# One encoder layer on one Trainium2 core: like turns of long and short matmuls joined, x brought in channel by channel, and the low weight parts laid 32 bytes further on

## The chip, the cores and the metric

The kernel runs on one core of one Trainium2 chip. The metric is the device time of one execution in microseconds (us). Before the change it is 1365.53 us, the median of 3 runs (1365.43 to 1365.78).

## What is computed

One layer over 256 tokens of 2048 channels in float32: RMSNorm, a bidirectional gated recurrence with its projections, RMSNorm and residual, then a gated feed-forward network with a width-3 convolution along the tokens, RMSNorm and residual. Cut to its matrix products and norms:

```python
h = rmsnorm(x, norm_pre_mix)                  # x: 256 x 2048
q, f_f, f_b, v, g = split(h @ w_in, 5)        # w_in: 2048 x 10240
o = recurrence_both_ways(silu(q), f_f, f_b, v)
m = (rmsnorm(o, g_norm) * silu(g)) @ w_out    # 2048 x 2048
x = x + rmsnorm(m, norm_post_mix)
h = rmsnorm(x, norm_pre_ffn)
up = dwconv3(h @ ffn_w_in, w_conv)            # 2048 x 11264
gate, val = split(up, 2)
x = x + rmsnorm((silu(gate) * val) @ ffn_w_out, norm_post_ffn)   # 5632 x 2048
```

## The kernel before, in words

**Weights and precision.** Every weight matrix is read once from HBM, in chunks of 512 output columns. A chunk comes in pieces of 4 tiles of 128 input rows (`raw`, 1 MB, line 115, issued on the SP queue) and is used in sub-chunks `s` of 2 such tiles (index `k`). Each float32 weight is split into two float32r parts: ScalarE rounds it to the high part `whi` (line 129), VectorE subtracts to get the low part `wlo` (line 130). `prep` does this three sub-chunks ahead (`LOOK`); four buffers of each part rotate, so a split waits until TensorE has finished with the sub-chunk four back. Activations are split alike: `xx[:, k, 0, :]` is the high and `xx[:, k, 1, :]` the low part of x for one tile of 128 channels and 256 tokens (`hh`, `oo` and `gg` are the same for later stages). A product is high by high, low by high and high by low.

**Two kinds of chunk.** `gemm` gives tokens as rows: the activations are the stationary operand, the weight parts move, and all its matmuls have 512 columns (lines 174, 177, 178). `gemm_t` gives channels as rows (the channel-row chunks: q and both f projections, and all but the first of the 22 up-projection chunks, 33 chunks in all): the weight parts are stationary. With the high weight part, both halves of the activation move at once, 512 columns (line 206, called **long** here); with the low weight part only the high half moves, 256 columns (line 209, **short**). A chunk has 64 long and 64 short ones. Before the change each of the first seven sub-chunks is a turn of 8 long and then 8 short matmuls, and the last one is four turns of 2 long and 2 short, so that the four output tiles are finished one after the other. The results collect in PSUM (`pg`, six banks) and are taken out by ScalarE and VectorE (lines 348, 349).

**The start.** SP issues a small parameter load, then pieces of x and of the first weights in turn (lines 247 to 260). x arrives with tokens as rows; TensorE transposes each tile of 128 by 128 (line 290, two for a tile of channels, 32 in all), ScalarE scales it by the norm weight into the high part (line 294), VectorE makes the low part (line 298). `split_x(0)` and `split_x(1)` stand ahead of the first chunk, the others between its sub-chunks. Ahead of all that, 18 transposes of the identity (line 269, `WARM`) keep TensorE busy. The mean square of x over channels is summed by ScalarE (8 squares with an accumulator, line 309), and spread over the partitions with two matmuls (`spread`, line 222).

**The order of the work.** A scheduler with a timeline model places the instructions on each engine, in-order queues; so the code's order is not always the queue's. Where two chunks meet, it mixes the last turns of one with the first of the next.

The lines that matter for the steps of the prediction: 115, 129, 130 (weights), 206, 209 (long, short), 269, 290, 294, 298 (start), 309 to 315 (mean square).

Of the kernel before, what the change touches and what calls it, by code (L numbers as in the profile page):

```python
# [11 lines left out]
F32 = mybir.dt.float32  # L12
F32R = mybir.dt.float32r
# [15 lines left out]
EPS = 1e-6  # L29
NLEV = 7  # L30
LOOK = 3
WARM = 18

ORDER = [(s, g) for g in range(NG - 1) for s in "qfbgv"][:-1]
ORDER += [("q", NG - 1), ("f", NG - 1), ("b", NG - 1), ("v", NG - 2), ("g", NG - 1), ("v", NG - 1)]
# [11 lines left out]
def encoder_layer(  # L47
    ctx: ExitStack,
    tc: tile.TileContext,
    x: bass.AP,  # L50
    w_in: bass.AP,
    w_o: bass.AP,
    w_up: bass.AP,
# [27 lines left out]
    r1 = const.tile([P, T], F32, name="rt", tag="rt")  # L81

    x_v = x.rearrange("(m p) d -> p m d", p=P)
    out_v = out.rearrange("(m p) d -> p m d", p=P)


# [31 lines left out]
    def prep(upto):  # L118
        while at["prep"] < min(upto, len(subs)):
            i = at["prep"]  # L120
            if at["load"] <= i:
                list(load())
            ci, s = subs[i]
            src = raws[ci, s // 2][:, 2 * (s % 2) : 2 * (s % 2) + 2, :]
            pl, sfx = (extra[0], str(s)) if ci == C_UP - 1 and s >= 2 * chunks[ci][2] - 4 else (wspl, "")
            hi = pl.tile([P, 2, 512], F32R, name="whi", tag="whi" + sfx)
            lo = pl.tile([P, 2, 512], F32R, name="wlo", tag="wlo" + sfx)
            for j in [slice(0, 1), slice(1, 2)] if i == 0 else [slice(0, 2)]:
                S.copy(hi[:, j], src[:, j])  # L129
                V.tensor_tensor(lo[:, j], src[:, j], hi[:, j].bitcast(F32), op=ALU.subtract)  # L130
            parts[ci, s] = (hi, lo)
            at["prep"] += 1
# [3 lines left out]
    def flush():  # L136
        while soon or later:
            step()
# [46 lines left out]
    def gemm_t(xx, need=None, pre=None):  # L185
# [4 lines left out]
        nsub = 2 * chunks[ci][2]  # L190
        base = subs.index((ci, 0))
        ps = [ps_g.tile([P, 2, T], F32, name="pg", tag="pg") for _ in range(4)]
        for s in range(nsub):
            if s == need:
                flush()
            if pre:
                pre(s)
            prep(base + s + (LOOK if ci else 1))
            hi, lo = parts[ci, s]


            tiles = [(n, 2 * s + j) for n in range(4) for j in range(2)]
            for run in [tiles] if s < nsub - 1 else [tiles[i : i + 2] for i in range(0, 8, 2)]:
                for n, k in run:
                    w = hi[:, k % 2, n * P : (n + 1) * P]
                    nc.tensor.matmul(ps[n], w, xx[:, k], start=(k == 0), stop=False)  # L206
                for n, k in run:
                    w = lo[:, k % 2, n * P : (n + 1) * P]
                    nc.tensor.matmul(ps[n][:, 0, :], w, xx[:, k, 0, :], start=False, stop=(k == 2 * nsub - 1))  # L209
            step()  # L210
        return ps

# [29 lines left out]
    hstack = ExitStack()  # L242
    sstack = ExitStack()
    spool = pool(sstack, "start", side="right")
    xs = spool.tile([P, 2, D], F32, name="xs")

    def load_x(a, b):
        nc.sync.dma_start(xs[:, :, a:b], x_v[:, :, a:b])

    nc.sync.dma_start(prm[:, :C_CW], par[:, :C_CW])  # L250
    load_x(0, 256)
    first = load(4)
    next(first), next(first)
    load_x(256, 512)
    list(first)
    load_x(512, 1024)
    list(load(2))
    load_x(1024, 1536)
    load_x(1536, 2048)
    make_identity(nc, ident)  # L260
    G.memset(mneg, -0.5)

# [20 lines left out]
    V.tensor_scalar(lb1, lb, -1.0, 1.0, op0=ALU.mult, op1=ALU.add)  # L283

    def split_x(k2):
        tp = ps_t.tile([P, 2, T], F32, name="tp", tag="tp")
        for j in range(2):
            k = 2 * k2 + j
            for m in range(2):
                nc.tensor.transpose(tp[:, j, m * P : (m + 1) * P], xs[:, m, k * P : (k + 1) * P], ident)  # L290
        for j in range(2):
            k = 2 * k2 + j
            w1 = prm[:, C_PRE + k : C_PRE + k + 1]
            S.activation(xx[:, k, 0, :], tp[:, j, :], AF.Copy, scale=w1)
        for j in range(2):
            k = 2 * k2 + j
            w1 = prm[:, C_PRE + k : C_PRE + k + 1]
            V.scalar_tensor_tensor(  # L298
                xx[:, k, 1, :], tp[:, j, :], w1, xx[:, k, 0, :].bitcast(F32), op0=ALU.mult, op1=ALU.subtract
            )  # L300

    ss1, rs1 = stile(8, "ss1"), stile(2, "rs1")

    def square_x(q):
        for m in range(2):
            jk = spool.tile([P, 512], F32, name="jk", tag="jk", bufs=2)
            i = 4 * m + q
            c = slice(q * 512, (q + 1) * 512)
            tc.keep_in_program_order(S.activation(jk, xs[:, m, c], AF.Square, accum_out=ss1[:, i : i + 1]))

    def mean_x():
        sx = stile(2, "sx")
        V.tensor_reduce(sx, ss1.rearrange("p (m q) -> p m q", q=4), axis=AX.X, op=ALU.add)
        rsqrt_mean(rs1, sx, D)
        soon.extend([nop, lambda: spread(rs1, r1)])

    split_x(0)
    split_x(1)
    ps0 = gemm_t(xx, pre=lambda s: split_x(s + 2) if 2 * s + 4 < KT else None)
    soon.extend([lambda q=q: square_x(q) for q in range(4)] + [mean_x])  # L320
    ps1 = gemm_t(xx)
    load_rest()
# [405 lines left out]
def _lay(inputs):  # L728
# [4 lines left out]
    def tiles(w):  # L733
# [17 lines left out]
    c = np.ascontiguousarray  # L751
    return {
        "x": c(f("x")[0]),
        "w_in": tiles(w_in),
        "w_o": tiles(w_o),
        "w_up": tiles(w_up),
# [21 lines left out]
```

## Time and profile before

| | |
|---|---|
| median of 3 runs | 1365.53 us |
| the profiled execution's own time | 1365.48 us |
| its span in the profile | 1363.7 us |
| TensorE matmuls | 7266, busy 1351.4 us (99%) |
| weight loads | 7266, busy 1167.3 us (86%) |
| VectorE, ScalarE busy | 955.5 us (70%), 698.0 us (51%) |
| HBM read | 245.63 MB, 182 GB/s over the span |
| mean granted TensorE clock | 0.998 |

The span is what the profile covers; 1.8 us of the execution's own time lie around it. A row of a timeline gives the start in us, the time from the first start to the last end, the engine (PE is TensorE's matmuls, PEld its weight loads, DVE VectorE, ACT ScalarE, POOL GpSimd, SPq the DMA queue of SyncE), the line, the operation, what it writes and reads, and how many in a row. The end of a matmul is modelled and reaches over the start of the next one, so the pace of a stream is read from one start to the next.

### The profile page before, as it was taken

The page shows a single profiled execution, that of the slowest core. Times are in us where ns is not written, and L with a number is a line of the kernel's source. Part 1 is how long each engine was busy: PE and PEld are TensorE (multiplying, and loading weights), DVE is VectorE, ACT ScalarE, POOL GpSimd, SP SyncE. Part 2 cuts the span into 40 slices and gives each one's busy share as a digit, 9 for nine tenths or more (in the row PEclk, how much of TensorE's full clock was granted, in tenths as well). Part 3 has the DMA queues.
Part 4 walks back from the last instruction along what each step waited for, and adds up shares of the span by engine and source line. Part 5 has one row for each costly group of instructions (what it writes and reads, how often), then busy time and mean ns, then how long its engine had stood idle before and what let it go on. Part 6 is the DMA issues. An engine that isn't in the chain of part 4 may idle for free.

```text
span 1363.7 us, 18236 instructions
## 1 busy us (share of the span) xinstructions
PE 1351.4 (99%) x7266; PEld 1167.3 (86%) x7266; DVE 955.5 (70%) x1204; ACT 698.0 (51%) x976; POOL 13.5 (1%) x21
## 2 busy tenths in 40 slices
PE   8999999999999999999999999999999999999997
PEld 7888988898898888888888888888888888888886
DVE  5688768876996887557767776777778675444444
ACT  5645545454545545547555555555555554434342
POOL 0000000000000000000000000000000000000000
PEclk9999999999999999999999999999999999999999
DMA  8554454445534534673555555555555556555552
GB/s 286 186 185 160 149 175 172 156 147 186 184 133 174 177 136 155 247 257 114 185 186 188 186 192 186 201 184 193 186 186 185 188 183 225 204 188 188 197 202 93
DMA packets 36997, 248.91 MB, mean 183 GB/s; under 512 B 4144, under 2 KB 4912, under 8 KB 7472
## 3 DMA queue, kind: packets, MB, share of 16 engines
q1 hardware_dynamic: 36912, 247.75, 51.8%
q8 instruction: 57, 0.93, 0.3%
q14 instruction: 28, 0.23, 0.0%
HBM read 245.63 MB, written 2.10 MB: 182 GB/s over the span
## 4 chain that ended last, share of the span: by engine, by line
PE 98%; DMA 1%; issue 0%; SPq 0%; DVE 0%; ACT 0%; DVEq 0%; POOLq 0%; POOL 0%
PE pg L206 35%; PE pg L209 18%; PE pg L174 13%; PE pg L178 13%; PE pg L177 13%; PE sc L462 3%; DMA raw<-in_w_in 1%; PE sc L428 1%; PE sc L519 1%; PE sc L487 1%; PE sc L518 1%; PE tp L233 0%; PE tp L614 0%; SPq L115 0%; DVE fw L715 0%
## 5 line engine op out<-in xcount | busy, mean ns | idle before, releaser
L130 DVE TENSOR_TENSOR wlo<-raw,whi 128x1024 fp32r<-128x1024 f32 (+1 forms) x457 | 556.3, 1221 | 342.2 <-ACT whi L129 334.4
L129 ACT CAST whi<-raw 128x1024 fp32r<-128x1024 f32 (+1 forms) x457 | 478.0, 1049 | 507.2 <-PE pg L178 227.1
L206 PE MATMUL pg<-hh,whi 128*128 128x512 f32 x1344 | 355.2, 393 | 0.0
L206 PEld LDWEIGHTS pg<-hh,whi 128*128 128x128 f32 x1344 | 234.1, 189 | 34.7
L209 PEld LDWEIGHTS pg<-hh,wlo 128*128 128x128 f32 x1344 | 197.4, 190 | 22.6
L206 PE MATMUL pg<-xx,whi 128*128 128x512 f32 x768 | 206.4, 397 | 0.3 <-DVE xx L298 0.3
L209 PE MATMUL pg<-hh,wlo 128*128 128x256 f32 x1344 | 203.3, 281 | 0.0
L206 PEld LDWEIGHTS pg<-xx,whi 128*128 128x128 f32 x768 | 134.8, 190 | 20.7 <-DVE xx L298 0.5
L174 PE MATMUL pg<-whi,gg 128*128 128x512 f32 x352 | 136.9, 389 | 0.0
L177 PE MATMUL pg<-wlo,gg 128*128 128x512 f32 x352 | 136.9, 389 | 0.0
L178 PE MATMUL pg<-whi,gg 128*128 128x512 f32 x352 | 136.9, 389 | 0.0
L209 PEld LDWEIGHTS pg<-xx,wlo 128*128 128x128 f32 x768 | 113.1, 190 | 12.3
L209 PE MATMUL pg<-xx,wlo 128*128 128x256 f32 x768 | 119.2, 283 | 0.0
L177 PE MATMUL pg<-wlo,xx 128*128 128x512 f32 x256 | 100.1, 391 | 0.0
L178 PE MATMUL pg<-whi,xx 128*128 128x512 f32 x256 | 100.0, 391 | 0.0
L174 PE MATMUL pg<-whi,xx 128*128 128x512 f32 x256 | 97.7, 390 | 0.0
L177 PEld LDWEIGHTS pg<-wlo,gg 128*128 128x128 f32 x352 | 66.1, 188 | 13.8
L178 PEld LDWEIGHTS pg<-whi,gg 128*128 128x128 f32 x352 | 66.1, 188 | 13.7
L174 PEld LDWEIGHTS pg<-whi,gg 128*128 128x128 f32 x352 | 66.1, 188 | 13.6
L178 PEld LDWEIGHTS pg<-whi,xx 128*128 128x128 f32 x256 | 48.1, 188 | 9.7
L177 PEld LDWEIGHTS pg<-wlo,xx 128*128 128x128 f32 x256 | 48.1, 188 | 9.8
L174 PEld LDWEIGHTS pg<-whi,xx 128*128 128x128 f32 x256 | 48.1, 188 | 9.7
(135 smaller groups left out, 1192.7 us busy)
## 6 DMA issues: line engine op xcount, KB each, us to landing
raw<-in_w_up SPq DMA_DIRECT2D x88, 1024.0 KB, 4.9
raw<-in_w_in SPq DMA_DIRECT2D x78, 1024.0 KB, 4.9
raw<-in_w_dn SPq DMA_DIRECT2D x44, 1024.0 KB, 4.9
raw<-in_w_o SPq DMA_DIRECT2D x16, 1024.0 KB, 4.9
x<-in_x SPq DMA_DIRECT2D x1, 2048.0 KB, 7.9
wp<-in_post SPq DMA_DIRECT2D x2, 1024.0 KB, 6.8
out<-fw SPq DMA_DIRECT2D x8, 256.0 KB, 2.6
xs<-in_x SPq DMA_DIRECT2D x3, 512.0 KB, 9.6
```

The costliest lines, as they stand in the source:

```text
L129: S.copy(hi[:, j], src[:, j])
L130: V.tensor_tensor(lo[:, j], src[:, j], hi[:, j].bitcast(F32), op=ALU.subtract)
L174: mm = nc.tensor.matmul(ps[m], a, hi[:, j, :], start=(k == 0), stop=False)
L177: nc.tensor.matmul(ps[m], a, lo[:, j, :], start=False, stop=False)
L178: nc.tensor.matmul(ps[m], b, hi[:, j, :], start=False, stop=(k == 2 * nsub - 1))
L206: nc.tensor.matmul(ps[n], w, xx[:, k], start=(k == 0), stop=False)
L209: nc.tensor.matmul(ps[n][:, 0, :], w, xx[:, k, 0, :], start=False, stop=(k == 2 * nsub - 1))
L428: nc.tensor.matmul(o, ones, a[:, i * 512 : i * 512 + 512], start=(j == 0), stop=(j == 1))
L462: nc.tensor.matmul(sc[:, j, :], kc[0][:, h, sl], r, start=True, stop=True)
L487: nc.tensor.matmul(sc[:, h, :], ks[:, d, h, s0 : s0 + P], qs[:, 1 - d, h, t0 : t0 + P], start=True, stop=True)
L518: nc.tensor.matmul(o[:, h, :], Sd[:, 2 * h + b, :], v[:, b, cs], start=True, stop=False)
L519: nc.tensor.matmul(o[:, h, :], So[1 - b][:, h, :], v[:, 1 - b, cs], start=False, stop=True)
```

## The change

The edits, in the order of the program:

- `WARM` goes from 18 to 24.
- The inputs have x a second time, laid out by channels on the host (`xt`: partition p holds channel 128k + p of every tile k, 256 tokens each). `xs` is loaded from it in pieces of tiles of channels (the same bytes as before), and `split_x` reads `xs` in SBUF: the 32 transposes of line 290 are gone. `split_x(0)` alone stands ahead of the first chunk; the others come between the sub-chunks, now behind `prep`.
- The mean square of x now has to be summed across partitions: four squares in place (ScalarE, 1024 elements a partition), four reductions over the 4 tiles of each and a fifth over the four results (VectorE), and two matmuls of one column with a vector of ones (TensorE).
- In `gemm_t` every second turn begins with its short matmuls, so that the short ones of two turns stand together, and then the long ones of the next two. In the first sub-chunk of all, the tiles go by `k`.
- The tile of the low weight part is 16 elements longer (4160 bytes in place of 4096), and in channel-row chunks the part begins 8 elements (32 bytes) in. This also moves what lies behind these tiles in SBUF.

```diff
-WARM = 18
+WARM = 24
...
-            lo = pl.tile([P, 2, 512], F32R, name="wlo", tag="wlo" + sfx)
+            lo = pl.tile([P, 1024 + 16], F32R, name="wlo", tag="wlo" + sfx)
+            o = 8 if ci < len(ORDER) and ORDER[ci][0] in "qfb" or C_UP < ci < C_UP + 2 * NJ else 0
+            lo = lo[:, o : o + 1024].rearrange("p (j n) -> p j n", n=512)
...
+        turn = [0]
         for s in range(nsub):
             if s == need:
                 flush()
+            prep(base + s + (LOOK if ci else 1))
             if pre:
                 pre(s)
-            prep(base + s + (LOOK if ci else 1))
             hi, lo = parts[ci, s]
             tiles = [(n, 2 * s + j) for n in range(4) for j in range(2)]
+            if ci == s == 0:
+                tiles.sort(key=lambda nk: nk[1])
             for run in [tiles] if s < nsub - 1 else [tiles[i : i + 2] for i in range(0, 8, 2)]:
-                for n, k in run:
-                    w = hi[:, k % 2, n * P : (n + 1) * P]
-                    nc.tensor.matmul(ps[n], w, xx[:, k], start=(k == 0), stop=False)
-                for n, k in run:
-                    w = lo[:, k % 2, n * P : (n + 1) * P]
-                    nc.tensor.matmul(ps[n][:, 0, :], w, xx[:, k, 0, :], start=False, stop=(k == 2 * nsub - 1))
+                long = turn[0] % 2 == 0
+                for kind in (long, not long):
+                    for n, k in run:
+                        w = (hi if kind else lo)[:, k % 2, n * P : (n + 1) * P]
+                        stop = s == nsub - 1 and kind != long and k == 2 * nsub - 1
+                        if kind:
+                            nc.tensor.matmul(ps[n], w, xx[:, k], start=(k == 0), stop=stop)
+                        else:
+                            nc.tensor.matmul(ps[n][:, 0, :], w, xx[:, k, 0, :], start=False, stop=stop)
+                turn[0] += 1
...
-    xs = spool.tile([P, 2, D], F32, name="xs")
+    xs = spool.tile([P, KT, T], F32, name="xs")
     def load_x(a, b):
-        nc.sync.dma_start(xs[:, :, a:b], x_v[:, :, a:b])
+        nc.sync.dma_start(xs[:, a:b], xt_v[:, a:b])
...
     def split_x(k2):
-        tp = ps_t.tile([P, 2, T], F32, name="tp", tag="tp")
...
+        for k in (2 * k2, 2 * k2 + 1):
+            S.activation(xx[:, k, 0, :], xs[:, k, :], AF.Copy, scale=prm[:, C_PRE + k : C_PRE + k + 1])
+        for k in (2 * k2, 2 * k2 + 1):
+            w1, hi = prm[:, C_PRE + k : C_PRE + k + 1], xx[:, k, 0, :].bitcast(F32)
+            V.scalar_tensor_tensor(xx[:, k, 1, :], xs[:, k, :], w1, hi, op0=ALU.mult, op1=ALU.subtract)
+    def square_x(q):
+        k = slice(4 * q, 4 * q + 4)
+        tc.keep_in_program_order(S.activation(xs[:, k], xs[:, k], AF.Square))
+        V.tensor_reduce(ss1[:, q, :], xs[:, k].rearrange("p k t -> p t k"), axis=AX.X, op=ALU.add)
+    def mean_x():
+        V.tensor_reduce(ss1[:, 4, :], ss1[:, :4].rearrange("p q t -> p t q"), axis=AX.X, op=ALU.add)
         tp = ps_t.tile([P, 2, T], F32, name="tp", tag="tp")
...
+            nc.tensor.matmul(tp[:, 0, m : m + 1], ss1[:, 4, m * P : (m + 1) * P], one, start=True, stop=True)
+        rsqrt_mean(rs1, tp[:, 0, :2], D)
...
     split_x(0)
-    split_x(1)
-    ps0 = gemm_t(xx, pre=lambda s: split_x(s + 2) if 2 * s + 4 < KT else None)
+    ps0 = gemm_t(xx, pre=lambda s: split_x(s + 1) if 2 * s + 2 < KT else None)
```

**What stands on TensorE at the start.** Before the change, from the first instruction on (`tp<-ident` are the warming transposes, `tp<-ident,xs` the transposes of x, `pg<-xx,whi` the long and `pg<-xx,wlo` the short matmuls of the first chunk):

```order
L269 MATMUL tp<-ident 128x128 x18
L290 MATMUL tp<-ident,xs 128x128 x8
L206 MATMUL pg<-xx,whi 128x512 x8
L209 MATMUL pg<-xx,wlo 128x256 x8
L206 MATMUL pg<-xx,whi 128x512 x8
L290 MATMUL tp<-ident,xs 128x128 x8
L209 MATMUL pg<-xx,wlo 128x256 x8
L206 MATMUL pg<-xx,whi 128x512 x4
L290 MATMUL tp<-ident,xs 128x128 x4
```

and after it:

```order
L283 MATMUL tp<-ident 128x128 x24
L220 MATMUL pg<-xx,whi 128x512 x8
L222 MATMUL pg<-xx,wlo 128x256 x16
L220 MATMUL pg<-xx,whi 128x512 x16
L222 MATMUL pg<-xx,wlo 128x256 x16
L220 MATMUL pg<-xx,whi 128x512 x16
```

The transposes of x have left the queue, and the second sub-chunk's short matmuls have moved ahead of its long ones.

**What stands on ScalarE at the start.** Before (`whi<-raw` is the high part of the weights, `xx<-tp` that of x, read from PSUM):

```order
L278 ACTIVATE lex<-lex 128x32
L129 CAST whi<-raw 128x512 x2
L294 ACTIVATE xx<-tp,prm 128x256 x4
L129 CAST whi<-raw 128x1024 x3
L294 ACTIVATE xx<-tp,prm 128x256 x6
L129 CAST whi<-raw 128x1024 x2
```

and after:

```order
L292 ACTIVATE lex<-lex 128x32
L301 ACTIVATE xx<-xs,prm 128x256 x2
L135 CAST whi<-raw 128x512 x2
L301 ACTIVATE xx<-xs,prm 128x256 x2
L135 CAST whi<-raw 128x1024
L301 ACTIVATE xx<-xs,prm 128x256 x4
L135 CAST whi<-raw 128x1024 x2
L301 ACTIVATE xx<-xs,prm 128x256 x8
```

x's high parts now stand ahead of the weights that they meet, eight of them ahead of the fifth sub-chunk's weights.

**What stands on TensorE in the middle of the up-projections.** Before, where two chunks meet and the plain turns of the second one begin (`hh` is the activation):

```order
L206 MATMUL pg<-hh,whi 128x512 x4
L209 MATMUL pg<-hh,wlo 128x256 x3
L206 MATMUL pg<-hh,whi 128x512 x4
L209 MATMUL pg<-hh,wlo 128x256 x4
L206 MATMUL pg<-hh,whi 128x512 x4
L209 MATMUL pg<-hh,wlo 128x256 x5
L206 MATMUL pg<-hh,whi 128x512 x8
L209 MATMUL pg<-hh,wlo 128x256 x8
```

and after, from the second run of a chunk to its last turns:

```order
L222 MATMUL pg<-hh,wlo 128x256 x8
L220 MATMUL pg<-hh,whi 128x512 x13
L222 MATMUL pg<-hh,wlo 128x256 x16
L220 MATMUL pg<-hh,whi 128x512 x16
L222 MATMUL pg<-hh,wlo 128x256 x16
L220 MATMUL pg<-hh,whi 128x512 x16
L222 MATMUL pg<-hh,wlo 128x256 x10
L220 MATMUL pg<-hh,whi 128x512 x4
L222 MATMUL pg<-hh,wlo 128x256 x4
```

Before, such a chunk has five runs of 8 and 8, four of 2 and 2, and four of about 4 and 4: 13 changes from short to long. After, its long runs are 7, 13, 16, 16, 4, 4 and 4: 7 changes.

More of the change, by code (lines that the diff above doesn't have):

```diff
@@ L50, in encoder_layer @@
     x: bass.AP,
+    xt: bass.AP,
     w_in: bass.AP,
@@ L83, in encoder_layer @@
     x_v = x.rearrange("(m p) d -> p m d", p=P)
+    xt_v = xt.rearrange("p (k t) -> p k t", t=T)
     out_v = out.rearrange("(m p) d -> p m d", p=P)
@@ L244, in encoder_layer @@
     spool = pool(sstack, "start", side="right")
-    xs = spool.tile([P, 2, D], F32, name="xs")
+    xs = spool.tile([P, KT, T], F32, name="xs")
     def load_x(a, b):
-        nc.sync.dma_start(xs[:, :, a:b], x_v[:, :, a:b])
+        nc.sync.dma_start(xs[:, a:b], xt_v[:, a:b])
     nc.sync.dma_start(prm[:, :C_CW], par[:, :C_CW])
-    load_x(0, 256)
+    load_x(0, 2)
     first = load(4)
     next(first), next(first)
-    load_x(256, 512)
+    load_x(2, 4)
     list(first)
-    load_x(512, 1024)
+    load_x(4, 8)
     list(load(2))
-    load_x(1024, 1536)
-    load_x(1536, 2048)
+    load_x(8, 12)
+    load_x(12, 16)
     make_identity(nc, ident)
@@ L285, in split_x @@
     def split_x(k2):
-        tp = ps_t.tile([P, 2, T], F32, name="tp", tag="tp")
[L287 to L300, printed above, removed]
@@ L302, in encoder_layer @@
-    ss1, rs1 = stile(8, "ss1"), stile(2, "rs1")
-    def square_x(q):
-        for m in range(2):
[L306 to L314, printed above, removed]
+        for k in (2 * k2, 2 * k2 + 1):
+            S.activation(xx[:, k, 0, :], xs[:, k, :], AF.Copy, scale=prm[:, C_PRE + k : C_PRE + k + 1])
@@ new lines, in split_x @@
+        for k in (2 * k2, 2 * k2 + 1):
+            w1, hi = prm[:, C_PRE + k : C_PRE + k + 1], xx[:, k, 0, :].bitcast(F32)
+            V.scalar_tensor_tensor(xx[:, k, 1, :], xs[:, k, :], w1, hi, op0=ALU.mult, op1=ALU.subtract)
+    ss1, rs1 = spool.tile([P, 5, T], F32, name="ss1"), stile(2, "rs1")
+    one = spool.tile([P, 1], F32, name="one")
+    G.memset(one, 1.0)
+    def square_x(q):
+        k = slice(4 * q, 4 * q + 4)
+        tc.keep_in_program_order(S.activation(xs[:, k], xs[:, k], AF.Square))
+        V.tensor_reduce(ss1[:, q, :], xs[:, k].rearrange("p k t -> p t k"), axis=AX.X, op=ALU.add)
@@ L753, in _lay @@
         "x": c(f("x")[0]),
+        "xt": c(f("x")[0].reshape(T, KT, P).transpose(2, 1, 0)).reshape(P, -1),
         "w_in": tiles(w_in),
```

## The prediction

> **What bounds the kernel now.** I read the page's busy table first, then the chain, then TensorE's timeline at the start and in the long stages.
>
> ```profile
> span 1363.7 us, 18236 instructions
> PE 1351.4 (99%) x7266; PEld 1167.3 (86%) x7266; DVE 955.5 (70%) x1204; ACT 698.0 (51%) x976; POOL 13.5 (1%) x21
> PE 98%; DMA 1%; issue 0%; SPq 0%; DVE 0%; ACT 0%; DVEq 0%; POOLq 0%; POOL 0%
> L130 DVE TENSOR_TENSOR wlo<-raw,whi 128x1024 fp32r<-128x1024 f32 (+1 forms) x457 | 556.3, 1221 | 342.2 <-ACT whi L129 334.4
> L129 ACT CAST whi<-raw 128x1024 fp32r<-128x1024 f32 (+1 forms) x457 | 478.0, 1049 | 507.2 <-PE pg L178 227.1
> ```
>
> The second row says that TensorE (PE) is busy 99% of the span, the third that 98% of the chain that ends last is TensorE's. The last two show the weight splits: VectorE's wait for ScalarE's, and ScalarE's wait for TensorE (227.1 us of their idle time for one line of its matmuls), not the reverse. So only two things can move the time: what TensorE does in a steady stream, and the start, where it waits. The start:
>
> ```profile
> 1.36 4.10 PE L269 MATMUL tp<-ident 128*128 128x128 f32 x18 [1.36 <-POOL ident masks.py:199]
> 1.64 0.93 SPq L115 DMA_DIRECT2D raw<-in_w_in  x2
> 2.62 0.43 SPq L248 DMA_DIRECT2D xs<-in_x  x1
> 5.25 0.87 PE L290 MATMUL tp<-ident,xs 128*128 128x128 f32 x4
> 6.11 1.31 ACT L129 CAST whi<-raw 128x512 fp32r<-128x512 f32 x2 [2.84 <-DMA raw<-in_w_in]
> 7.32 0.83 ACT L294 ACTIVATE xx<-tp,prm 128x256 fp32r<-128x256 f32 x2
> 8.67 0.63 PE L290 MATMUL tp<-ident,xs 128*128 128x128 f32 x4 [2.55 <-DMA xs<-in_x]
> 9.05 3.63 PE L206 MATMUL pg<-xx,whi 128*128 128x512 f32 x8
> 12.48 1.18 PE L209 MATMUL pg<-xx,wlo 128*128 128x256 f32 x8
> ...
> 13.54 1.05 ACT L129 CAST whi<-raw 128x1024 fp32r<-128x1024 f32 x1 [2.26 <-DMA raw<-in_w_in]
> 14.83 1.05 ACT L129 CAST whi<-raw 128x1024 fp32r<-128x1024 f32 x1 [0.24 <-DMA raw<-in_w_in]
> ...
> 23.23 1.12 PE L209 MATMUL pg<-xx,wlo 128*128 128x256 f32 x8
> 24.18 0.60 PE L290 MATMUL tp<-ident,xs 128*128 128x128 f32 x4
> 24.54 2.09 PE L206 MATMUL pg<-xx,whi 128*128 128x512 f32 x8
> ...
> 28.34 0.60 PE L290 MATMUL tp<-ident,xs 128*128 128x128 f32 x4
> 28.70 1.17 PE L206 MATMUL pg<-xx,whi 128*128 128x512 f32 x4
> ```
>
> The first long matmul starts only at 9.05, because the transposes ahead of it in the queue wait for the second piece of x (8.67). The eight then take 3.43 us to the next start, 0.43 each. The granted clock says why (the columns are the stretch, its length, busy time of PE, PEld, DVE, ACT and POOL, the clock, DMA):
>
> ```profile
> 8.00:9.00 1.00, 0.33 (x3) 0.36 (x4) 0.95 (x3) 0.15 (x1) 0.00 (x0) 1.00 1.03 355
> 11.00:12.00 1.00, 1.00 (x3) 0.76 (x3) 0.76 (x2) 0.28 (x1) 0.00 (x0) 0.50 0.99 399
> ```
>
> The clock is halved while TensorE works off its first eight. The steady pace, from the up-projections and the last stage:
>
> ```profile
> 719.04 2.00 PE L206 MATMUL pg<-hh,whi 128*128 128x512 f32 x8
> 720.89 1.12 PE L209 MATMUL pg<-hh,wlo 128*128 128x256 f32 x8
> 721.84 2.00 PE L206 MATMUL pg<-hh,whi 128*128 128x512 f32 x8
> ...
> 733.01 0.63 PE L206 MATMUL pg<-hh,whi 128*128 128x512 f32 x2
> 733.48 0.39 PE L209 MATMUL pg<-hh,wlo 128*128 128x256 f32 x2
> 733.71 0.63 PE L206 MATMUL pg<-hh,whi 128*128 128x512 f32 x2
> ...
> 735.80 1.09 PE L206 MATMUL pg<-hh,whi 128*128 128x512 f32 x4
> 736.73 0.63 PE L209 MATMUL pg<-hh,wlo 128*128 128x256 f32 x4
> ...
> 741.41 2.00 PE L206 MATMUL pg<-hh,whi 128*128 128x512 f32 x8
> 1116.03 0.40 PE L174 MATMUL pg<-whi,gg 128*128 128x512 f32 x1
> ...
> 1349.30 0.39 PE L174 MATMUL pg<-whi,gg 128*128 128x512 f32 x1
> 1349.53 0.39 PE L177 MATMUL pg<-wlo,gg 128*128 128x512 f32 x1
> 1349.75 0.39 PE L178 MATMUL pg<-whi,gg 128*128 128x512 f32 x1
> ...
> 1355.19 0.39 PE L178 MATMUL pg<-whi,gg 128*128 128x512 f32 x1
> L174 PE MATMUL pg<-whi,gg 128*128 128x512 f32 x352 | 136.9, 389 | 0.0
> ```
>
> In the last stage, with nothing but 512 columns, each matmul follows the one before by 0.22 to 0.23 us; from the first start to the last are 239.16 us, and the last row counts 352 of each of the three lines, so 239.16/1055 = 0.2267. In a chunk of turns a long one costs more. Runs of 8 take 1.85 (0.231 each), of 4 take 0.93, of 2 take 0.47 (0.235 each). So the first two after a short run cost 0.47, the next two 0.46, the last four 0.92. The excess sits behind the change from short to long and fades out. Short ones go the other way: 2 take 0.23 (0.115 each), 8 take 0.95, the last of them at 0.120.
>
> **The start, term by term.** The transposes go, and the long matmuls no longer stand behind the second piece of x. I follow the new order with durations of the rows. The first high weight part is ready at 6.11 + 1.31/2 = 6.77; x's first two high parts read SBUF as soon as the first piece lands (before 5.25) and are ready earlier. Eight long ones at 0.23 from 6.8 end at 8.6, the eight short ones at 9.6. Now TensorE waits: the second piece of x lands at 8.67, its two high parts take 0.83 (to 9.5), the second sub-chunk's weights 1.05 on ScalarE and about 1.23 on VectorE, so to 11.8. Short, then long: to 14.6. The third sub-chunk's weights land at 13.54 and are split at 14.6, so its long ones follow at once, to 16.45; 16 short ones to 18.35; the fourth one's long ones to 20.2. The fifth sub-chunk (x's last eight high parts stand ahead of its weights on ScalarE: 14.83 + 1.05 + 8 x 0.42 + 1.05 = 20.3) begins at about 20.2 to 20.3.
>
> Before, the same point is the row at 24.54. That is 4.3 us. The last transposes, 28.34 to 28.70, make it 4.7; the two one-column matmuls for the sum over channels cost at most what a transpose does, together 0.2. So 4.5. A piece of x is now 128 runs of 2 KB and not 256 of 1 KB; the second piece took 6.0 us from issue to use (2.62 to 8.67), the weights ahead of it 4.5 (1.64 to 6.11). If it gained all of that 1.5 us, TensorE would still meet the weights at 13.54; I take 0.4. The six more warming transposes cover 6 x 0.21 us in which TensorE waits anyway. **The start: -4.9 us**, between -2.8 (the clock halved once more, below) and -6.4 (the 1.5 us in full).
>
> Hidden are the squares and sums. VectorE gets five reductions of 1024 elements, ScalarE four squares for eight. A pass over 1024 elements takes 1.22 us on VectorE and 1.50 with the stride of the dearest row:
>
> ```profile
> L417 DVE TENSOR_TENSOR pr<-ks,qs 128x1024 f32<-128x1024 f32 x4 | 6.0, 1502 | 0.0
> 34.00:56.00 22.00, 22.00 (x130) 19.41 (x129) 11.74 (x14) 14.61 (x29) 0.71 (x1) 1.00 0.56 196
> ```
>
> In the 22 us of the second chunk VectorE is busy 11.74; 7.5 us more fit, and the low parts queued behind them are not what TensorE waits for (the rows of lines 130 and 129 above). If that lead is gone, TensorE waits for the rest, a rival below. The load of the masks now waits in SP's queue for that sum's matmul, with the next weights behind it; the sum comes in the second chunk's seventh turn, when those loads would only just be due.
>
> **The joining.** Against 0.2267 and 0.120 apiece, a pair of runs 8 + 8 (721.84 - 719.04 = 2.80 against 2.773) has an excess of about 0.02 us, one of 2 + 2 (0.70 against 0.693) 0.004, one of 4 + 4 (5.61/4 = 1.40 against 1.387) 0.014. Before, a chunk is 5, 4 and 4 of these: 5 x 0.02 + 4 x 0.004 + 4 x 0.014 = 0.17; from 719.04 to 741.41 it is 22.37 against 22.19, so 0.18. After, four long runs of 7 to 16 and three of 4: 4 x 0.02 + 3 x 0.014 = 0.12, if a run of 16 has no more excess than one of 8, as the fading says. 0.06 x 33 chunks: **-2.0 us**, between 0 (the excess goes by matmuls, not by changes) and -3 (runs of 4 among longer ones cost as those of 2).
>
> [...]
>
> **The 32 bytes.** No row shows a part at another phase. From below: all the excess that is left goes, 0.12 x 33 = -4.0; or the shorts run on at the 0.115 of a run of two, 2112 x 0.005 = -10.6. From above: a short pays what a long one pays behind a short run, 0.235 - 0.227 = 0.008, times 2112 = +17. The nearest row is the last stage's, where high and low parts, as moving data, keep the same pace (L174, L177, L178): **0**. VectorE writes the shifted part as before, and the splits wait for TensorE.
>
> **The sum.** 1365.5 - 4.9 - 2.0 = 1358.6 us, made against the execution of 1365.48, which is 0.05 from the median of the runs.
>
> **The rivals.**
>
> *The clock is halved again.* In the new start TensorE waits from about 9.6 to 11.8. Before, its wait from 6.12 to 8.67 was followed by the half clock. If this one is too, up to 3.4 us of work go at half pace: 1.7 us, 1360.3. For it: the gap is nearly as long. Against: work before and after it is denser. [...] The trace had the half clock behind 2.55 us, so I keep it.
>
> *The shorts speed up.* If the 32 bytes part the reads of weights and data that make a short one cost 0.120 and not 0.115: 1358.6 - 10.6 = 1348. For it: a short one just behind a long run is quicker with the same columns. Against: nothing shows that the phase is why.
>
> *The shift hurts, and the kernel is slower.* Each short's weight load meets its data worse, at the +0.008 above: 1358.6 + 17 = 1375.5. It decides from 0.0033 us for each of 2112 shorts, which eats the 6.9. Against: the pace does not depend on which of the four buffers is read.
>
> *The sum over channels is late.* Its matmuls stand in TensorE's queue behind five reductions; if VectorE's lead is short by three of them, TensorE waits 3.7 to 4.5 us: 1362.3 to 1363.1. For it: the second chunk is where they all fall. Against: the 11.74 of 22 us.
>
> *The joining does nothing*, the excess going by matmuls: 1360.6.
>
> **How the numbers follow.** Forecast 0.56, half clock 0.12, quicker shorts 0.14, shift hurts 0.07, late sum 0.06, no joining 0.05. The range takes in the quicker shorts at its lower end and the the half clock and the late sum's middle at its upper end: 1348 to 1362.7. About 0.2% (2.7 us) is what a measurement of this kernel can tell from no change; so faster ends at 1362.8. The forecast, the half clock, the quicker shorts and no joining lie below that (0.87), and 0.01 of the late sum: faster 0.88; the rest of the late sum: same 0.05; the shift's harm: slower 0.07.
>
> **What would show it.** The first long matmul at about 6.8 and not 9.05; the first of the fifth sub-chunk near 20.2; no half clock after 6 us. In the up-projections 16 and 16 in 5.57 us, the chunk of 22.37 at 22.31. A short run whose steady pace is not 0.120 tells what the 32 bytes do, either way. The prediction is wrong if TensorE waits for anything behind the first 20 us, or if the steady pace of long or short ones changes.

## The result, and the profile after

| | before | after |
|---|---|---|
| median (range) | 1365.57 us (1365.24 to 1366.29), 6 runs | 1371.93 us (1370.34 to 1372.27), 6 runs |
| ratio of the times | | 1.0042, 95% interval 1.0033 to 1.0052 |
| the profiled execution: own time, span | 1365.48, 1363.7 us | 1371.97, 1370.2 us |

The kernel became 6.4 us slower; 1358.6 us with a range up to 1362.7 was forecast. The prediction is wrong in sign.

The page of the changed kernel, first its totals, then the chain of waits by engine, then two groups (busy time, mean ns of one, and behind the second bar the idle time before it with its releaser):

```profile
span 1370.2 us, 18096 instructions
PE 1357.9 (99%) x7244; PEld 1164.2 (85%) x7244; DVE 965.1 (70%) x1208; ACT 699.4 (51%) x964; POOL 12.4 (1%) x22
PE 98%; DMA 0%; issue 0%; DVE 0%; ACT 0%; SPq 0%; DVEq 0%; POOLq 0%; POOL 0%; ACTq 0%
...
L135 ACT CAST whi<-raw 128x1024 fp32r<-128x1024 f32 (+1 forms) x457 | 478.2, 1049 | 516.2 <-PE pg L184 237.5
...
L222 PE MATMUL pg<-xx,wlo 128*128 128x256 f32 x768 | 109.9, 283 | 2.5 <-DVE wlo L136 2.5
```

TensorE has 22 matmuls fewer and is busy 6.5 us longer (1351.4 before). The chain is still 98% TensorE, ScalarE still waits for TensorE, and TensorE's only sizeable wait behind its first matmul is one of 2.5 us for low weight parts. So no wait came in: the stream of matmuls itself is slower. Where, TensorE's timeline shows (start, time to the last end, line, what it writes and reads, how many):

```profile
6.51 2.19 PE L220 MATMUL pg<-xx,whi 128*128 128x512 f32 x8
8.54 1.09 PE L222 MATMUL pg<-xx,wlo 128*128 128x256 f32 x8
12.12 1.21 PE L222 MATMUL pg<-xx,wlo 128*128 128x256 f32 x8 [2.48 <-DVE wlo L136]
13.17 5.42 PE L220 MATMUL pg<-xx,whi 128*128 128x512 f32 x16
18.43 2.04 PE L222 MATMUL pg<-xx,wlo 128*128 128x256 f32 x16
20.31 3.84 PE L220 MATMUL pg<-xx,whi 128*128 128x512 f32 x16
...
649.25 0.39 PE L220 MATMUL pg<-hh,whi 128*128 128x512 f32 x1
1118.85 0.39 PE L180 MATMUL pg<-whi,gg 128*128 128x512 f32 x1
...
1239.68 0.39 PE L180 MATMUL pg<-whi,gg 128*128 128x512 f32 x1
...
1242.91 0.39 PE L184 MATMUL pg<-whi,gg 128*128 128x512 f32 x1
...
1361.63 0.39 PE L184 MATMUL pg<-whi,gg 128*128 128x512 f32 x1
```

The last four rows are the last stage. From its first start to its last it took 239.16 us before and takes 1361.63 - 1118.85 = 242.78 now, with the same 1056 matmuls in the same order. Before, a matmul followed the one before it by 0.2267; between the rows at 1239.68 and 1242.91 lie 14 steps, 0.231 each. The up-projections (649.25 to 1118.85) take 469.60; before, they took 1116.03 - 645.05 = 470.98 (before's two rows: one shown with the prediction, and this one):

```profile
645.05 0.39 PE L206 MATMUL pg<-hh,whi 128*128 128x512 f32 x1
```

The whole difference by stages, from such first starts:

| stretch | before | after | difference |
|---|---|---|---|
| span's start to the 33rd long matmul (the fifth sub-chunk) | 24.54 | 22.16 | -2.38 |
| from there to the channel-row up-projections | 620.51 | 627.09 | +6.58 |
| channel-row up-projections | 470.98 | 469.60 | -1.38 |
| last stage | 239.16 | 242.78 | +3.62 |
| behind it | 8.5 | 8.6 | +0.1 |

The first and third rows are the gains that the change was costed with, in part. The second and fourth are the loss, 10.2 us, and they hold all the chunks with tokens as rows: v, g, the output projection, the first up chunk and the last stage. The second also holds the 12 channel-row chunks of the recurrence, but by the trace's steps its 1248 token-row matmuls take 5.95 us more and the channel-row ones 0.3. So 9.6 of the 10.2 us lie in chunks in which the offset is zero.

### The profile page after: what moved, and what is told of

Same layout as the page of the kernel before. It is cut to its first block, busy times and chain, and to the rows that moved or that the text cites. A ratio compares the mean times of both kernels' runs of the same rounds, so it can differ in the third digit from the quotient of the medians.

```text
span 1370.2 us, 18096 instructions
## 1 busy us (share of the span) xinstructions
PE 1357.9 (99%) x7244; PEld 1164.2 (85%) x7244; DVE 965.1 (70%) x1208; ACT 699.4 (51%) x964; POOL 12.4 (1%) x22
## 4 chain that ended last, share of the span: by engine, by line
PE 98%; DMA 0%; issue 0%; DVE 0%; ACT 0%; SPq 0%; DVEq 0%; POOLq 0%; POOL 0%; ACTq 0%
PE pg L220 36%; PE pg L222 18%; PE pg L180 13%; PE pg L183 13%; PE pg L184 13%; PE sc L467 3%; PE sc L433 1%; PE sc L524 1%; PE sc L523 1%; PE sc L492 1%; DMA raw<-in_w_in 0%; PE tp L247 0%; PE tp L619 0%; ACT whi L135 0%; DVE fw L720 0%
## 5 line engine op out<-in xcount | busy, mean ns | idle before, releaser
L136 DVE TENSOR_TENSOR wlo<-raw,whi 128x1024 fp32r<-128x1024 f32 (+1 forms) x457 | 556.1, 1221 | 336.8 <-ACT whi L135 334.4
L220 PE MATMUL pg<-hh,whi 128*128 128x512 f32 x1344 | 333.6, 393 | 0.0
L220 PEld LDWEIGHTS pg<-hh,whi 128*128 128x128 f32 x1344 | 242.4, 188 | 44.4
L220 PE MATMUL pg<-xx,whi 128*128 128x512 f32 x768 | 195.5, 397 | 0.0
L222 PEld LDWEIGHTS pg<-hh,wlo 128*128 128x128 f32 x1344 | 179.1, 188 | 12.7
L222 PE MATMUL pg<-hh,wlo 128*128 128x256 f32 x1344 | 182.8, 280 | 0.0
L220 PEld LDWEIGHTS pg<-xx,whi 128*128 128x128 f32 x768 | 139.1, 190 | 25.8 <-issue 0.4
L222 PEld LDWEIGHTS pg<-xx,wlo 128*128 128x128 f32 x768 | 104.5, 188 | 10.3 <-DVE wlo L136 2.7
L222 PE MATMUL pg<-xx,wlo 128*128 128x256 f32 x768 | 109.9, 283 | 2.5 <-DVE wlo L136 2.5
```

What stands on the lines that cost most here:

```text
L220: nc.tensor.matmul(ps[n], w, xx[:, k], start=(k == 0), stop=stop)
```

## The theory and its rival

**By addresses.** How fast one matmul follows the other depends on where weight parts and activations lie in SBUF against each other. The change moves more than the 32 bytes say. Addresses in a partition, modulo 256 (called phase below; a shift of 256 bytes leaves the mean step at 0.2283 in experiment 5, one of 128 takes the up-projections from 469.7 to 473.8 in experiment 10), as the built programs have them:

| tile | before | after |
|---|---|---|
| `xx`, `hh`, `oo` | 224 | 224 |
| `gg` | 224 | 160 |
| `whi`, four buffers | 224 | 160 |
| `wlo`, four buffers | 224 | 160, 96, 32, 224; 32 more in channel-row chunks |

Before, everything stood at one phase, since all these tiles are multiples of 256 bytes long. (Four more pairs of buffers serve the last sub-chunks of the output projection alone and are left out here.) The low part's tile is 4160 bytes long now, so each buffer lies 64 bytes further on. And `ss1` (8 floats) and `sx` (2) have left the pool of small tiles ahead of the weights, which moves everything behind it by 64 bytes.

**By the order** (the rival). The joined turns or the new splits of x disturb later stages, and the token-row chunks pay for it.

## The experiments

The times of before on the same chip lie at 1365.42 (first four), 1365.24 (next four) and 1365.16 (last four). A ratio is given where more than one run was timed. Mean steps are taken from the traces, start to next start.

**1. The tile's longer size and the offset taken out.** Everything else as in the changed kernel.

```diff
-            lo = pl.tile([P, 1024 + 16], F32R, name="wlo", tag="wlo" + sfx)
-            o = 8 if ci < len(ORDER) and ORDER[ci][0] in "qfb" or C_UP < ci < C_UP + 2 * NJ else 0
+            lo = pl.tile([P, 1024], F32R, name="wlo", tag="wlo" + sfx)
+            o = 0
```

> The changed kernel with the low part's tile at 4096 bytes again and no offset; high and low parts then share one address modulo 256, but both still lie 64 bytes off the activations' (160 against 224), since the change also took 40 bytes of statistics from the pool ahead of the weights. Theory A (TensorE's pace hangs on the addresses of the two operands to each other; the change broke an even layout): between 1361 and 1372 us, nearer to whichever of the two shifts counts more. Theory B (the 32 bytes of offset alone do the harm): about 1361, which is the time before less 2.6 at the start and less 2 for the joining. Theory C (the joined order is slower by itself): 1372, as changed.

1364.54 us (1362.69 to 1365.10, 11 runs), ratio 0.9989 (0.9980 to 0.9998). All weights and `gg` stand at 160 now, `xx`, `oo` and `hh` at 224. TensorE's timeline:

```profile
101.13 0.39 PE L183 MATMUL pg<-wlo,xx 128*128 128x512 f32 x1
...
103.93 0.39 PE L180 MATMUL pg<-whi,xx 128*128 128x512 f32 x1
...
648.58 0.40 PE L220 MATMUL pg<-hh,whi 128*128 128x512 f32 x1
1114.96 0.40 PE L180 MATMUL pg<-whi,gg 128*128 128x512 f32 x1
1354.13 0.39 PE L184 MATMUL pg<-whi,gg 128*128 128x512 f32 x1
```

The last stage is back at 1354.13 - 1114.96 = 239.17: `gg` and both parts are at one phase again, though not at the old one, so what counts is the distance and not the address. A token-row chunk of the recurrence, where weights and `xx` lie 64 bytes apart, is slow: 12 steps in 2.80, 0.233 each; over all 768 matmuls of the v and g chunks the mean is 0.2346, against 0.2282 before. And the up-projections with the same 64 bytes are **faster**, 466.38: what harms the one kind of chunk helps the other.

**2. The offset alone taken out** (`o = 0`, the longer tile kept).

```diff
-            o = 8 if ci < len(ORDER) and ORDER[ci][0] in "qfb" or C_UP < ci < C_UP + 2 * NJ else 0
+            o = 0
```

> The changed kernel with the 4160-byte tiles kept and the offset set to zero in all chunks. Theory A (addresses): the token-row chunks stay as slow as in the changed kernel, about 2304 matmuls at 230 to 233 ns for 227, so 1370 us or more. Theory B (the offset alone): about 1361. Theory C (the order): 1372.

1369.46 us (1368.83 to 1371.00, 6 runs), ratio 1.0031 (1.0019 to 1.0042).

```profile
12.94 3.84 PE L220 MATMUL pg<-xx,whi 128*128 128x512 f32 x16
16.62 2.03 PE L222 MATMUL pg<-xx,wlo 128*128 128x256 f32 x16
...
646.97 0.39 PE L220 MATMUL pg<-hh,whi 128*128 128x512 f32 x1
1115.71 0.40 PE L180 MATMUL pg<-whi,gg 128*128 128x512 f32 x1
1358.50 0.39 PE L184 MATMUL pg<-whi,gg 128*128 128x512 f32 x1
```

The last stage is 242.79 as in the changed kernel: the loss there is the tile's length, not the offset. The up-projections are 468.74, by 0.86 shorter than with the offset. The first two rows are for the start: here 16 long matmuls take 3.68, and the expected 1370 or more was missed by 0.5.

**3. The old addresses with the new order.** As 1, and two unused small tiles put the 64 bytes back.

```diff
-    ss1, rs1 = spool.tile([P, 5, T], F32, name="ss1"), stile(2, "rs1")
+    ss1, rs1 = spool.tile([P, 5, T], F32, name="ss1"), stile(2, "rs1"); stile(8, "gap1"), stile(8, "gap2")
```

> The changed kernel's order and start, with every tile of weights and activations at the address modulo 512 that it had before the change: 4096-byte tiles, no offset, 64 bytes put back ahead of the weights. Theory A (addresses) and theory B (the offset): the token-row chunks at 226.7 ns again, and 1361 us (1365.5 less 2.6 at the start, less 2 for the joining). Theory C (the order): 1372.

1361.35 us (1360.63 to 1362.55, 7 runs), ratio 0.9970 (0.9959 to 0.9981). All tiles are at 224.

```profile
642.96 0.39 PE L220 MATMUL pg<-hh,whi 128*128 128x512 f32 x1
1112.69 0.40 PE L180 MATMUL pg<-whi,gg 128*128 128x512 f32 x1
1351.85 0.39 PE L184 MATMUL pg<-whi,gg 128*128 128x512 f32 x1
```

The last stage is 239.16, to the hundredth that of before, and the up-projections begin 6.29 us earlier than in the changed kernel with the same start (33rd long matmul at 22.14). The order does no harm; with the addresses of before it wins 4.1 us by the medians.

**4. The longer tile alone, in the kernel before.**

```diff
-            lo = pl.tile([P, 2, 512], F32R, name="wlo", tag="wlo" + sfx)
+            lo = pl.tile([P, 1024 + 16], F32R, name="wlo", tag="wlo" + sfx)[:, :1024].rearrange("p (j n) -> p j n", n=512)
```

> The kernel before with nothing but the low part's tile at 4160 bytes, so that its four buffers lie at four addresses modulo 256; order on every engine unchanged, no offset. Theory A (addresses): slower, the token-row chunks losing 3 to 6 ns on each of 2304 matmuls (7 to 14 us): 1372 to 1380 us. Theories B and C: 1365.5, as before.

1373.37 us (1373.02 to 1374.78, 5 runs), ratio 1.0058 (1.0044 to 1.0072). Modulo 256 nothing that the last stage reads moves but three of the four low buffers, and the kernel is 8 us slower: 3.6 in the last stage, 4.4 between the start and the up-projections, 0.15 in the up-projections (the profiled execution's start, with a longer half clock, took another 1.1).

```profile
1121.66 0.40 PE L174 MATMUL pg<-whi,gg 128*128 128x512 f32 x1
...
1240.66 0.40 PE L177 MATMUL pg<-wlo,gg 128*128 128x512 f32 x1
1240.90 0.39 PE L178 MATMUL pg<-whi,gg 128*128 128x512 f32 x1
1241.12 0.39 PE L174 MATMUL pg<-whi,gg 128*128 128x512 f32 x1
...
1364.45 0.39 PE L178 MATMUL pg<-whi,gg 128*128 128x512 f32 x1
```

The last stage is 242.79. The low part's matmul of line 177 here takes 0.24 to the next start, the high part's of line 178, whose buffers did not move, 0.22. These three rows are not the whole: over the stage the low ones' mean step is 0.2320 (0.2270 before), and the high ones lose too, 0.2292 (0.2265). Even sub-chunks that read the one low buffer that stayed at 224 run at 0.2301; their 12 steps come back to 0.2267 only in the last three. So a step depends also on the phases of the matmuls ahead of it, not on its own two operands alone.

This run also lays `gg` 256 bytes further on against the high parts. That this does nothing, experiment 5 shows: it moves `xx` by 256 bytes against the weights, and the v and g chunks keep their step (0.2283, as in experiment 3).

**5. `hh` 64 bytes further on.** Experiment 1 says that channel-row chunks gain from 64 bytes and token-row chunks lose; so the weights stay at 224 and only the activation of the up-projections moves (as 3, and the tile that `hh` shares with `xx` is 64 elements longer).

```diff
-    hh = acts.tile([P, KT, 2, T], F32R, name="hh", tag="xx")
+    hh = acts.tile([P, KT * 2 * T + 64], F32R, name="hh", tag="xx")[:, 16 : 16 + KT * 2 * T].rearrange("p (k i t) -> p k i t", i=2, t=T)
```

> The run with the old addresses, in which only the activation tile of the up-projections (hh) is laid 64 bytes further on, so that the 21 channel-row chunks of that stage have weights and activations 64 bytes apart, as in the run without pad (there the stage took 466.4 us, with the old addresses 469.7), while all token-row chunks but the first up-projection chunk keep equal addresses. Theory A (the distance between the two operands' addresses sets the pace, and channel-row and token-row chunks want different distances): the stage at 466.4, the first up-projection chunk's 96 matmuls 0.6 us slower, so 1361.35 - 3.3 + 0.6 = 1358.7. Rival (the 3.3 us of that run came from the weights' place itself, not from their distance to the activations): 1361.4.

1358.01 us (1357.81 to 1359.50, 5 runs), ratio 0.9949 (0.9937 to 0.9962).

```profile
641.84 0.40 PE L220 MATMUL pg<-hh,whi 128*128 128x512 f32 x1
...
700.47 1.98 PE L222 MATMUL pg<-hh,wlo 128*128 128x256 f32 x16
702.28 3.82 PE L220 MATMUL pg<-hh,whi 128*128 128x512 f32 x16
705.94 1.34 PE L222 MATMUL pg<-hh,wlo 128*128 128x256 f32 x10
...
1108.29 0.40 PE L180 MATMUL pg<-whi,gg 128*128 128x512 f32 x1
```

The up-projections are 466.45, as in experiment 1, by a different address and the same distance. The 16 short matmuls from 700.47 take 1.81, 0.113 each, the 10 from 705.94 to the next long one at 707.12 take 0.118 each. Over all 21 chunks the mean step behind a short one is 0.1165 (0.1193 in experiment 3), behind a long one 0.2297 (0.2294): the gain is in the short ones.

**6. The start without the early short matmuls.** As 3, and the second sub-chunk keeps long ahead of short.

```diff
-                long = turn[0] % 2 == 0
+                long = turn[0] % 2 == 0 or ci == 0 and s < 2
```

> The run with the old addresses, in which the second sub-chunk of the first chunk begins with its long matmuls again, so that TensorE's one wait of 2.5 us becomes two of about 1 us. Theory D (the changed start lost 1.8 us to a half clock behind that wait, in most executions): no half clock, the fifth sub-chunk at 20.3 and not 22.1, 1359.6 us. [...]

1360.48 us (1360.08 to 1360.55, 5 runs), ratio 0.9963 (0.9951 to 0.9976).

```profile
10.58 2.14 PE L220 MATMUL pg<-xx,whi 128*128 128x512 f32 x8 [0.49 <-ACT whi L135]
...
20.23 2.11 PE L220 MATMUL pg<-xx,whi 128*128 128x512 f32 x8 [0.38 <-ACT whi L135]
...
641.20 0.39 PE L220 MATMUL pg<-hh,whi 128*128 128x512 f32 x1
1110.92 0.40 PE L180 MATMUL pg<-whi,gg 128*128 128x512 f32 x1
```

The long matmuls need only the high part, which is ready 1.2 us ahead of the low one (VectorE's pass for a low part takes 1221 ns on average in the changed kernel). The wait of 2.5 us falls into shorter ones (0.49 in the first row), no clock is halved (it is 1.00 in every microsecond from 9 to 15), and the times of the five runs lie within 0.5 us (those of 3 within 1.9). The median is only 0.9 below that of 3, where 1.8 was expected; three of 3's seven runs lie at 1360.6 to 1361.1, so they probably had no half clock.

**7. The 32 bytes alone, in all chunks.** As 3, with unused tiles that put all four low buffers at 0, 32 bytes behind 224.

```diff
-            hi = pl.tile([P, 2, 512], F32R, name="whi", tag="whi" + sfx)
+            hi = pl.tile([P, 2, 512], F32R, name="whi", tag="whi" + sfx); i or pl.tile([P, 8], F32R, name="gap", tag="gap1", bufs=1)
...
-            lo = pl.tile([P, 1024], F32R, name="wlo", tag="wlo" + sfx)
+            lo = pl.tile([P, 1024], F32R, name="wlo", tag="wlo" + sfx); i or pl.tile([P, 56], F32R, name="gap", tag="gap2", bufs=1)
```

> The run with the old addresses, in which the low weight parts alone lie 32 bytes further on, in all chunks, at one address modulo 256 for all four buffers; everything behind them is back in place. Theory A (distance sets the pace): the token-row chunks' matmuls with the low part slower by 3 to 6 ns, and with the steps to it and from it 2 to 4 ns on each of 2304, 5 to 9 us; the channel-row stage (469.7) changes by less than 1.5 either way: 1366 to 1371 us. Rival (only distances of 64 bytes or more count): 1361.4. Rival (the 32 bytes help the channel-row chunks as the change's name has it): that stage at 467 or less.

1376.12 us (1374.93 to 1376.98, 5 runs), ratio 1.0078 (1.0064 to 1.0092).

```profile
649.10 0.40 PE L220 MATMUL pg<-hh,whi 128*128 128x512 f32 x1
1119.62 0.40 PE L180 MATMUL pg<-whi,gg 128*128 128x512 f32 x1
...
1365.79 0.39 PE L184 MATMUL pg<-whi,gg 128*128 128x512 f32 x1
```

The last stage takes 246.17, 7.0 more than at one phase. The up-projections, the chunks that the offset was laid into, take 470.52 against 469.73 in 3: there too 32 bytes cost, they gain nothing. The whole lies 5 us above the upper end of what was expected: the token-row chunks lose 13 us and not 5 to 9, for the high parts' steps, at 224 as ever, grow too (0.2320 in the last stage, 0.2265 before).

This run also bears on another rival: that other engines or transfers, working in SBUF at the same time, slow TensorE down. Near the end of the last stage TensorE works alone for 3.2 us, but for one transfer of 0.02 MB (columns as in the prediction's windows: five engines' busy time, clock, DMA share, GB/s). The first row is this run, the second the kernel before:

```profile
1357.40:1360.60 3.20, 3.20 (x15) 2.62 (x14) 0.00 (x0) 0.00 (x0) 0.00 (x0) 1.00 0.02 5
1347.10:1350.10 3.00, 3.00 (x15) 2.49 (x14) 0.00 (x0) 0.00 (x0) 0.00 (x0) 1.00 0.00 0
```

The steps in the first are 0.231, 0.233 and 0.236 in turn, in the second 0.226 to 0.227. So the loss is there with VectorE, ScalarE and GpSimd at rest, next to no transfers and the full clock.

**8. Experiments 5 and 6 together.** Both edits above.

> The run with the old addresses with both edits, hh 64 bytes further on and the second sub-chunk long matmuls first. Theories A and D: 1361.35 - 2.7 - 1.8 = 1356.9 us, faster than both kernels. If the two do not add, 1358.7 to 1361.

1357.68 us (1357.33 to 1357.88, 5 runs), ratio 0.9943 (0.9930 to 0.9955): faster than both kernels, though 0.8 us short of the sum of the two expected gains, with 466.51 for the up-projections:

```profile
641.62 0.40 PE L220 MATMUL pg<-hh,whi 128*128 128x512 f32 x1
1108.13 0.40 PE L180 MATMUL pg<-whi,gg 128*128 128x512 f32 x1
```

**9 to 11. Other distances for `hh`.** As 8, with `hh` 8, 32 or 48 elements on (32, 128 or 192 bytes) in place of 16; one run each.

```diff
-    hh = acts.tile([P, KT * 2 * T + 64], F32R, name="hh", tag="xx")[:, 16 : 16 + KT * 2 * T].rearrange("p (k i t) -> p k i t", i=2, t=T)
+    hh = acts.tile([P, KT * 2 * T + 64], F32R, name="hh", tag="xx")[:, 8 : 8 + KT * 2 * T].rearrange("p (k i t) -> p k i t", i=2, t=T)
```

> The best run so far (both edits) with hh 32 bytes, not 64, further on. What is looked at is the up-projections' channel-row stage in the profile: 469.7 us at a distance of 0, 466.5 at 64. Theory A with a gain that grows with the distance up to 64: between, about 468. Theory A with steps of 64: 469.7. A loss, as with the 32 bytes on the low part alone (470.5): above 470.

> The same with hh 128 bytes further on. If addresses count modulo 128: 469.7 in the channel-row stage, and the first up-projection chunk's matmuls at 227 and not 233 ns. If modulo 256: some other value, near 466.5 if every distance but 0 helps.

> The same with hh 192 bytes further on, 64 the other way modulo 256. If modulo 128: 466.5, as at 64. If the sign counts: another value, up to a loss.

1363.32, 1364.90 and 1359.21 us. The up-projections, with the mean steps behind a long and a short matmul from the trace, beside the two distances that were timed above:

| `hh` further on by | up-projections | a long one | a short one |
|---|---|---|---|
| 0 (experiments 3, 6) | 469.7 | 0.2294 | 0.1193 |
| 32 | 471.6 | 0.2332 | 0.1169 |
| 64 (experiments 5, 8) | 466.5 | 0.2297 | 0.1165 |
| 128 | 473.8 | 0.2331 | 0.1187 |
| 192 (64 the other way) | 468.2 | 0.2329 | 0.1146 |

64 bytes the one way and the other differ by 1.7 us, so the sign of the distance counts. A period of 128 bytes is out: 128 is the worst and not like 0, nor near 466.5, as it would be if every distance but 0 helped. Single runs, so differences below some 0.5 us say nothing here.

**12. Not joined.** As 3, and every turn goes long, then short, as before the change: what is left is x by channels.

```diff
-                long = turn[0] % 2 == 0
+                long = True
...
-                        stop = s == nsub - 1 and kind != long and k == 2 * nsub - 1
+                        stop = not kind and k == 2 * nsub - 1
```

> The run with the old addresses without the joining: every turn long, then short, as before the change; x still by channels. The joining took 1.27 us off the 21 channel-row chunks of the up-projections (470.99 to 469.72), so 2.0 over all 33, but in the first chunk it also made TensorE wait and the clock halve in most executions (1.8). Theory: the channel-row stage at 471.0, no half clock at the start, 1361.5 us, within 1 us of the run with the joining. Rival (the joining is worth nothing): 1359.6.

1361.49 us (1361.18 to 1361.85, 9 runs), ratio 0.9973 (0.9963 to 0.9983).

```profile
20.12 2.11 PE L220 MATMUL pg<-xx,whi 128*128 128x512 f32 x8 [0.23 <-ACT whi L135]
...
641.03 0.39 PE L220 MATMUL pg<-hh,whi 128*128 128x512 f32 x1
1112.02 0.40 PE L180 MATMUL pg<-whi,gg 128*128 128x512 f32 x1
```

The up-projections are 470.99, as before the change (470.98); against 6 (469.72), whose start has no half clock either, the joining is worth 1.27 us in these 21 chunks: the long steps fall from 0.2312 to 0.2294, which is 2.4 us, and the short ones rise from 0.1185 to 0.1193, which takes 1.1 back. At the start it brings the one wait of 2.49 us that in experiment 3 came with the half clock, so with the whole change's order it nets nothing: 1361.35 against 1361.49.

## Why the prediction was wrong, point by point

**The failed step: "The 32 bytes ... 0".** It took the nearest row, the last stage, where high and low parts keep the same pace. But there both parts stood at the same phase as `gg`, so that row could not show what another phase does; nor could "the pace does not depend on which of the four buffers is read" speak against harm, since all four were at 224. Besides, only the 32 bytes in the channel-row chunks were costed. The front part says that the longer tile moves what lies behind it; the prediction gave that no term, nor the 40 bytes dropped ahead of the weights, and these two are the larger part: 8.4 us of the loss, against 1.4 for the term that was put at 0. From experiment 3 to the changed kernel the profiled spans grow from 1360.4 to 1370.2, 9.8 us, and the experiments between them part that: the 64 bytes of the dropped tiles 2.3 (3 to 1), the tile's length 6.1 (1 to 2: 4.3 of span and 1.8 because 2's profiled start had no half clock), the offset 1.4 (2 to after: 3.2 less the 1.8, the difference in when the fifth sub-chunk begins, 20.32 to 22.16). By medians it is 3.2, 4.9 and 2.5; the half clock seems to have fallen into unlike shares of the runs.

```text
span, profiled executions      us
before                         1363.7
x by channels, the start       -2.4   (-4.2 without the half clock)
joining                        -1.0   (12 to 6: 1359.7 to 1358.7)
addresses                      +9.8
sum                            1370.1   (measured 1370.2)
```

That addresses alone cost time, experiment 4 shows: 242.79 for 239.16 in one stage, with only the phases of low weight parts changed. Whether it is the reads of weights and data that meet, no run shows.

**The rival "the shift hurts"** had the sign, and for the wrong reason. It put +17 us on the short matmuls. Those are no slower in the changed kernel (0.1181 a step in the up-projections, against 0.1185 before and 0.1193 in experiment 3); the loss sits in the token-row chunks, whose matmuls all have 512 columns. Its chance of 0.07 was small for something on which no row of the trace bore.

**The quicker shorts** exist, but not by the 32 bytes: 64 bytes between weights and activation bring the mean step from 0.1193 to 0.1165 and the kernel 3.3 us (5 against 3, 1361.35 - 1358.01). The place of the excess was guessed right, the distance was not.

**The start.** The first long matmul came at 6.51 (6.8 forecast). The wait ended at 12.12 (11.8). Two pieces of the chain of waits (start, length, what) say why:

```profile
3.53 6.15 DMA raw<-in_w_in
...
10.84 1.24 DVE wlo L136
```

The second sub-chunk's weights landed at 9.68, and their low part was ready at 12.08. The forecast had let them be there in time and counted from x, so that 11.8 came out near is luck. The wait was forecast as 2.2 us long and was 2.48, and the half clock came. The windows of the changed kernel (length, busy time of five engines, then the granted clock):

```profile
14.00:15.00 1.00, 1.00 (x3) 0.73 (x3) 0.55 (x3) 1.00 (x2) 0.00 (x0) 0.50 1.06 438
17.00:18.00 1.00, 1.00 (x6) 0.79 (x6) 1.00 (x4) 1.00 (x3) 0.00 (x0) 1.00 0.97 399
```

The 16 long matmuls from 13.17 took 5.26 us to the next start, where experiment 2, without the half clock, took 3.68 for the same. That is 1.6 us, near the rival's price of 1.7; its chance of 0.12 was too low. Without the half clock the fifth sub-chunk begins at 20.3 (2, the same order), 20.2 (6) and 20.1 (12), as forecast; with it, at 22.16. The half clock came with waits of 2.45 (experiment 1), 2.48 (the changed kernel), 2.49 (3) and 2.55 us (before). With waits of 1.64 (2) and 2.09 us (5) it did not come. Four of six runs of the changed kernel are at 1371.9 to 1372.3 and two at 1370.34, so most of them probably had it.

Two small slips stand in the prediction's sums, and neither decides anything here. The bounds of the start treat its 0.4 us unlike: -2.8 leaves it out (4.9 less 1.7 is 3.2), and -6.4 counts it twice (with the 1.5 us in full it is 6.0). And the excesses of the joining by its own rows are 0.027, 0.007 and 0.015 us, not 0.02, 0.004 and 0.014, so 2.3 us and not 2.0.

**The joining** is 1.27 us in 21 chunks, 0.06 each, just as worked out; but over all it is 1.0 and not 2.0, for the 12 chunks of the recurrence's stage show nothing of it (from the fifth sub-chunk to the up-projections it is 620.91 in 12 and 620.96 in 6). Why these gain nothing, no run shows.

**The squares and sums** are hidden as said, though a reduction costs 2.0 us and not 1.22 to 1.50. The groups of the changed kernel:

```profile
L313 DVE TENSOR_REDUCE ss<-xs 128x256 f32<-128x1024 f32 x4 | 8.1, 2022 | 0.0
...
L319 PE MATMUL tp<-one,ss 128*128 128x1 f32 x4 | 0.5, 229 | 0.0
```

The matmuls of line 319 wait 0.0 us; the rival of the late sum did not come.

## What to carry to other kernels

A diff that adds or drops a few bytes in a pool moves every tile behind it: work out the addresses of the operands that meet in TensorE before and after, and give the move a term of its own. A row in which all operands stand at one phase is no evidence on what another phase costs, so a wide price from both sides should keep weight on both signs. And where an order lets an engine begin with what is ready first (here the high parts), one long wait becomes several short ones; here that kept the clock from being halved (waits of 0.49, 0.35 and 0.38 us in experiment 6, for one of 2.49 in 3).

## What the runs showed of the hardware

- In these runs the step from one matmul to the next depends on the distance of stationary and moving data modulo 256 bytes, with a sign, and unlike for the two kinds of chunk. In the v and g chunks, where 512 columns of weights move over a stationary activation, the mean is 0.2283 us at distance 0 (experiment 3) and 0.2346 at 64 (1); in the last stage 0.2267 at 0 and 0.2333 with the low parts alone at 32 (7). With weights stationary, of five distances tried `hh` 64 bytes further on is best (466.5 for the stage) and 128 worst (473.8). Moving both operands by 64 bytes changes nothing (239.17 against 239.16), nor does moving one by 256 (0.2283 in 3 and 5). A change of phase lingers: some nine steps after it the pace of 0.2267 is back (4). The loss needs no other engine at work and next to no transfers (steps of 0.231 to 0.236 at 5 GB/s in 7). What in the chip makes it so, no run here shows.
- At the start the half clock (a granted clock of 0.50) lasts 3.41 us (13.50 to 16.91 in the changed kernel, 9.21 to 12.62 before) and costs about half of that (1.6 us: 5.26 for 3.68 over the same 16 long matmuls). In the profiled executions it came with waits of 2.45 to 2.55 us and not with 1.64 or 2.09. In experiment 4, where TensorE stands idle through all of 7 to 8 us, it lasted about 6.8 (a mean clock of 0.88 in 7 to 8, 0.50 in 9 to 10 and in 12 to 13, 0.70 in 14 to 15). The times of the changed kernel lie in two groups 1.6 to 1.9 us apart (two at 1370.34, four at 1371.90 to 1372.27).
